# Two hybrid decoder layers on one core: the recurrence begun with its x groups and computed in pairs of tiles, all weight splits on VectorE, P normalised by ScalarE

## The chip, the core and the metric

The kernel runs on one core of a Trainium2 chip. A core has five engines, each with an instruction queue of its own that is worked through in order: TensorE (PE, matmuls; PEld is its weight load), VectorE (DVE), ScalarE (ACT), GpSimd (POOL) and SyncE (SP), which here issues the weight DMAs. They meet through semaphores. The metric is the device time of one execution in microseconds.

## The reference

Two layers of a hybrid decoder run over 264 columns: a prompt of 256 positions and 8 single-step samples. One layer:

```
h = rmsnorm(x);  z = h @ w_in                       # 2048 -> 4096 columns
attn  = sliding-window attention, 16 heads, 4 kv heads, rotary, window 128, a sink per head
lru   = RG-LRU(conv4(x_branch)) * gelu(gate_branch) # 512 wide
sconv = B * conv3(C * h_in)                         # 512 wide
x = x + concat(rmsnorm(attn), rmsnorm(lru), rmsnorm(sconv)) @ w_out
x = x + SwiGLU(rmsnorm(x))                          # 5632 wide
```

The recurrence is `h[t] = a[t]*h[t-1] + sqrt(1-a[t]^2)*i[t]*xc[t]`, with `a` and `i` from sigmoid gates (two small matmuls on the convolved branch `xc`). The attention's probabilities are `p = exp(s - m) / (sum(exp(s - m)) + exp(sink - m))`. Besides the output, the new states of the recurrence, the convolutions and the key and value caches are returned.

## The kernel before

Features lie on partitions in 128-row tiles, the 264 columns in the free dimension. A product with a weight is kept near fp32 by splitting both factors in a high and a low half: three matmuls a tile (`hi*xh`, `hi*xl`, `lo*xh`, lines L152 to L154). Weights stream in as 720 tiles `raw` of 128x1024 (512 KB, five buffers), 360 a layer: 64 for w_in, 32 for w_out, then gate/up and down in three chunks. Each is split: ScalarE casts `hi` (L118), then VectorE subtracts to get `lo` (L122); for 20 of each layer's tiles, every third from 14 to 71, GpSimd does it (L120). Up to four split tiles stand ahead of the product; a split can start when the product has released the buffer four tiles back. One weight tile feeds 24 matmuls, called a block here.

w_in is worked through in 16 groups of four blocks, in the order of `GROUPS` (L41): k, v, the four q heads sets with x and g groups between them, four c groups (the short convolution's C and h), two b groups. A group's result in PSUM is evacuated by VectorE with its RMS scale (`evac`), and starts side work: `attn(i, 0)` and `attn(i, 1)` for each q group (scores L599/L600, maxima L604, Exp L618, P times 1/sum L626, transposes L632, P times V L641/L643), `decode` for the samples, `gelu` and then `lru(c)` for each of the two tiles of a g group, `sconv` for a c group, and `mixnorm` (a norm, then scale and split to the halves `Ba`, `Bl`, `Bs` that w_out reads). Side work is written as generators in queues; after every block `pull` takes one step of each, so `yield n` sets how many blocks later the next step is issued. The four `lru(c)` run one after another, 264 columns at a time, from the x groups' `uxe` and the constants `lsm` (`lru_consts`, a chain of small instructions on four columns). A scheduler then orders each engine's instructions by their dependences and expected times; the rows below show the order that results. w_out (4 groups of 8 blocks) reads `Ba` (attention, k 0 to 7), `Bl` (recurrence, 8 to 11) and `Bs` (short convolution, 12 to 15), in this order. A norm is a sum of squares (`acc`, added up by GpSimd in L186, the short convolution's by VectorE), a product with ones on TensorE (L196), then Ln and Exp on ScalarE and a Newton step on VectorE (L198 to L210).

ScalarE's functions stand in table sets: Ln and Exp of the norm in one, Tanh in another, with a table load (ACT_TABLE_LOAD) where they alternate.

Of the kernel before, what the change touches and what calls it, by code (L numbers as in the profile page):

```python
# [14 lines left out]
P = 128  # L15
# [40 lines left out]
class Kern:  # L56
# [54 lines left out]
    def _split(self):  # L111
# [24 lines left out]
    def linear(self, ngroups, halves, G, xk, evac, alternate=False, before=None):  # L136
        nc = self.nc
        kk = 8 // G
        last = halves * kk - 1
        for g in range(ngroups):  # L140
            ps = [self.MM(alternate and g % 2, j) for j in range(G)]
            for h in range(halves):
# [91 lines left out]
    def run(self):  # L234
# [17 lines left out]
        self.on_pool = {360 * l + j for l in range(DEPTH) for j in range(14, 72, 3)}  # L252
# [14 lines left out]
        self.qp = Queue()  # L267
        self.qbd = self.pers.tile([P, 2, NS, 32], F32, tag="qbd", name="qbd")
# [19 lines left out]
    def prep(self, ks, g, st):  # L288
        """Split x * g for the tiles ks of the next product; their squares go to st."""
# [98 lines left out]
    def mixer(self, l, st, head):  # L388
# [18 lines left out]
        nc.gpsimd.memset(M.che[:, :, 0:2], 0.0)  # L407
# [23 lines left out]
        def setup(ps):  # L431
# [26 lines left out]
            self.lru_consts(l)  # L458
            yield 1
# [13 lines left out]
        def evac(g, ps):  # L473
# [110 lines left out]
    def attn(self, i, p, slot):  # L584
# [119 lines left out]
    def lru_consts(self, l):  # L704
        nc = self.nc
        m = self.lsm
# [19 lines left out]
        self.hba, self.hbi, self.sp2 = hba, hbi, s2  # L726
# [8 lines left out]
    def gelu(self, c, ps):  # L735
# [4 lines left out]
        nc.vector.tensor_tensor(out=t, in0=u, in1=u, op=OP.mult)  # L740
# [259 lines left out]
```

## Time and profile before

| | |
|---|---|
| three runs | 2244.34, 2248.47, 2250.54 us; median 2248.47 |
| profiled execution | span 2247.6 us (the page gives no other time of it) |
| TensorE busy | 2192.0 us (98%) |
| VectorE, ScalarE, GpSimd busy | 1364.4 (61%), 1022.1 (45%), 244.3 us (11%) |
| matmuls, weight loads | 17810 each |
| weight splits | 720 casts on ScalarE; 680 subtractions on VectorE, mean 1235 ns; 40 on GpSimd |
| DMA | 398.33 MB, mean 177 GB/s |

The span runs from the first to the last instruction. A group's row gives the line, the engine, what it writes and reads with the shape, the count, the busy time and the mean of one, and behind the bar the idle time of the engine before it with what ended it. The mixer of layer 0 lies between about 40 and 260 us, that of layer 1 between about 1140 and 1365 us; the rest is w_out and the feed-forward part. The clock column is the clock granted to TensorE, as a share of 2.4 GHz; the lower level is 1.2 GHz.

### The profile page before, as it was taken

What the parts mean: (1) busy time and instruction counts of PE and PEld (TensorE: products, weight loads), DVE (VectorE), ACT (ScalarE), POOL (GpSimd) and SP (SyncE); (2) the same over time, 40 slices, a digit from 0 to 9 for tenths busy, and PEclk for the clock granted to TensorE, in tenths of its full rate; (3) what the DMA queues carried; (4) which work ended last, traced back from release to release, by engine and by line L of the source; (5) the groups of instructions that cost most, each with busy time, mean ns of one, the idle gap of its engine ahead of it and who ended that gap; (6) DMA issues with size and microseconds to landing.
All of it is one profiled execution on the core that took longest, in us unless ns stands there. A gap on an engine that the chain in (4) does not pass through costs nothing.

```text
span 2247.6 us, 42700 instructions
## 1 busy us (share of the span) xinstructions
PE 2192.0 (98%) x17810; PEld 2163.0 (96%) x17810; DVE 1364.4 (61%) x2172; ACT 1022.1 (45%) x1436; POOL 244.3 (11%) x233
## 2 busy tenths in 40 slices
PE   8999899999999999999999899999999999999997
PEld 7989799999999999999999789999999999999997
DVE  7679865555455554555665897565654556545554
ACT  5566554444334443344544665454433444334443
POOL 4324320000000000000123242100000000000002
PEclk9999899999999999999999999999999999999998
DMA  8644555556555555665565345555555555555553
GB/s 294 202 138 128 151 174 186 183 179 180 180 184 179 180 179 184 199 178 180 181 228 170 123 124 170 181 179 184 178 181 182 182 180 179 180 183 181 179 181 102
DMA packets 111617, 398.33 MB, mean 177 GB/s; under 512 B 13312, under 2 KB 15872, under 8 KB 110400
## 3 DMA queue, kind: packets, MB, share of 16 engines
q1 hardware_dynamic: 109840, 389.57, 54.9%
q0 software_dynamic: 864, 4.94, 0.5%
q8 instruction: 139, 2.28, 0.4%
q10 hardware_dynamic: 720, 1.10, 0.1%
q14 instruction: 54, 0.44, 0.1%
HBM read 385.82 MB, written 7.10 MB: 175 GB/s over the span
## 4 chain that ended last, share of the span: by engine, by line
PE 90%; DVE 8%; ACT 1%; DMA 1%; issue 0%; POOL 0%; SPq 0%; DVEq 0%; ACTq 0%
PE mm L152 20%; PE mm L153 20%; PE mm L154 20%; PE pb L154 5%; PE pa L152 5%; PE pa L153 5%; PE pb L152 5%; PE pa L154 4%; PE pb L153 4%; DVE lo L122 1%; DVE Ba L626 1%; DVE Ba L217 1%; DVE lwv L785 0%; DVE la L786 0%; PE pb L632 0%; ACT hi L118 0%
## 5 line engine op out<-in xcount | busy, mean ns | idle before, releaser
L122 DVE TENSOR_TENSOR lo<-raw,hi 128x1024 fp32r<-128x1024 f32 x680 | 838.9, 1235 | 769.4 <-ACT hi L118 769.1
L118 ACT CAST hi<-raw 128x1024 fp32r<-128x1024 f32 x720 | 752.4, 1047 | 991.2 <-PE mm L153 609.1
L152 PE MATMUL mm<-A,hi 128*128 128x264 f32 x2432 | 704.4, 290 | 7.2 <-ACT hi L118 7.2
L154 PE MATMUL mm<-A,lo 128*128 128x264 f32 x2432 | 695.6, 286 | 3.6 <-DVE lo L122 3.6
L153 PE MATMUL mm<-A,hi 128*128 128x264 f32 x2432 | 695.7, 286 | 0.7 <-DVE A L217 0.7
L152 PEld LDWEIGHTS mm<-A,hi 128*128 128x128 f32 x2432 | 462.4, 190 | 15.9 <-issue 8.3
L154 PEld LDWEIGHTS mm<-A,lo 128*128 128x128 f32 x2432 | 461.8, 190 | 6.3 <-DVE lo L122 5.4
L153 PEld LDWEIGHTS mm<-A,hi 128*128 128x128 f32 x2432 | 463.3, 191 | 2.2 <-DVE A L217 1.3
L152 PE MATMUL mm<-Ba,hi 128*128 128x264 f32 x896 | 257.3, 287 | 3.2 <-DVE tab L524 3.2
L154 PE MATMUL mm<-Ba,lo 128*128 128x264 f32 x896 | 257.0, 287 | 3.4 <-DVE lo L122 3.4
L186 POOL TENSOR_TENSOR acc<-acc,t 128x264 f32<-128x264 f32 x79 | 80.3, 1017 | 1651.8 <-ACT t L185 1640.7
L153 PE MATMUL mm<-Ba,hi 128*128 128x264 f32 x896 | 257.2, 287 | 0.0
L152 PE MATMUL pa<-A,hi 128*128 128x264 f32 x704 | 201.4, 286 | 0.0
L154 PE MATMUL pa<-A,lo 128*128 128x264 f32 x704 | 200.5, 285 | 0.0
L154 PE MATMUL pb<-A,lo 128*128 128x264 f32 x704 | 200.4, 285 | 0.0
L153 PE MATMUL pa<-A,hi 128*128 128x264 f32 x704 | 200.2, 284 | 0.0
L152 PE MATMUL pb<-A,hi 128*128 128x264 f32 x704 | 200.1, 284 | 0.0
L153 PE MATMUL pb<-A,hi 128*128 128x264 f32 x704 | 199.9, 284 | 0.0
L154 PEld LDWEIGHTS mm<-Ba,lo 128*128 128x128 f32 x896 | 170.6, 190 | 3.9 <-DVE lo L122 3.8
L152 PEld LDWEIGHTS mm<-Ba,hi 128*128 128x128 f32 x896 | 170.6, 190 | 3.6 <-DVE tab L524 3.6
L153 PEld LDWEIGHTS mm<-Ba,hi 128*128 128x128 f32 x896 | 170.5, 190 | 0.1
L153 PEld LDWEIGHTS pa<-A,hi 128*128 128x128 f32 x704 | 133.8, 190 | 0.0
(263 smaller groups left out, 3324.7 us busy)
## 6 DMA issues: line engine op xcount, KB each, us to landing
raw<-in_wg SPq DMA_DIRECT2D x352, 512.0 KB, 3.6
raw<-in_wd SPq DMA_DIRECT2D x176, 512.0 KB, 3.6
raw<-in_wi SPq DMA_DIRECT2D x128, 512.0 KB, 3.8
raw<-in_wo SPq DMA_DIRECT2D x64, 512.0 KB, 3.8
Bs<-in_kc SPq DMA_DIRECT2D x2, 1024.0 KB, 6.3
out_sk<-Bs POOLq DMA_DIRECT2D x2, 1024.0 KB, 8.4
Bl<-in_vc SPq DMA_DIRECT2D x2, 1024.0 KB, 8.4
q<-t SPq DMA_DIRECT2D x32, 64.0 KB, 2.0
```

The costliest lines, as they stand in the source:

```text
L118: self.nc.scalar.copy(hi, raw)
L122: self.nc.vector.tensor_tensor(out=lo, in0=raw, in1=hi.bitcast(F32), op=OP.subtract)
L152: nc.tensor.matmul(o, hi[:, c:c + P], xh, start=kt == 0, stop=False)
L153: nc.tensor.matmul(o, hi[:, c:c + P], xl, start=False, stop=False)
L154: nc.tensor.matmul(o, lo[:, c:c + P], xh, start=False, stop=kt == last)
L186: (eng or nc.gpsimd).tensor_tensor(out=st["acc"], in0=st["acc"], in1=q, op=OP.add)
L217: self.nc.vector.scalar_tensor_tensor(out=lo, in0=x, scalar=g, in1=hi.bitcast(F32), op0=OP.mult, op1=OP.subtract)
L626: nc.vector.tensor_scalar(pt[g][:, sl], pt[g][:, sl], es[:, c:c + 1], None, OP.mult)
```

## The change

- `GROUPS`: each x group now stands ahead of a q group (k v x q x q g q g q, then c and b), and `lru` starts with the x group, not with the g group behind it.
- `lru(i)` computes two tiles at once: 528 columns an instruction where the form allows it, the two reciprocals and scans apart. It writes `h` to a tile of its own (`lh`); the product with gelu and the square for the norm move to `gelu`'s second half.
- w_out takes its k tiles in another order (`OUT_ORDER`): the recurrence's first, then the attention's, then the short convolution's, and waits only for the two it needs.
- No split on GpSimd: all 720 `lo` on VectorE.
- P is multiplied by 1/sum on ScalarE, and so are gelu's square and the first taps of both convolutions computed there.
- `lru_consts` gets two buffers; layer 1's is issued in the feed-forward part of layer 0, and is free to go anywhere before.

```diff
-GROUPS = [("k", 0), ("v", 0), ("q", 0), ("x", 0), ("q", 1), ("x", 1), ("q", 2), ("g", 0), ("q", 3), ("g", 1),
+GROUPS = [("k", 0), ("v", 0), ("x", 0), ("q", 0), ("x", 1), ("q", 1), ("g", 0), ("q", 2), ("g", 1), ("q", 3),
           ("c", 0), ("c", 1), ("c", 2), ("c", 3), ("b", 0), ("b", 1)]
+OUT_ORDER = (4, 5, 0, 1, 2, 3, 6, 7)
...
-        if j in self.on_pool:
-            self.nc.gpsimd.tensor_tensor(out=lo, in0=raw, in1=hi.bitcast(F32), op=OP.subtract)
-        else:
-            self.nc.vector.tensor_tensor(out=lo, in0=raw, in1=hi.bitcast(F32), op=OP.subtract)
+        self.nc.vector.tensor_tensor(out=lo, in0=raw, in1=hi.bitcast(F32), op=OP.subtract)
...
+        order = order or range(halves)
+        first, last = order[0] * kk, order[-1] * kk + kk - 1
         for g in range(ngroups):
             ps = [self.MM(alternate and g % 2, j) for j in range(G)]
-            for h in range(halves):
+            for h in order:
...
-        self.on_pool = {360 * l + j for l in range(DEPTH) for j in range(14, 72, 3)}
...
-            self.until(lambda: all(k in self.ready for k in range(2 * h + 2)))
+            self.until(lambda: 2 * h in self.ready and 2 * h + 1 in self.ready)
         self.sides.append(self.qp)
-        self.linear(4, 8, 4, self.bh, evac_out, alternate=True, before=before)
+        self.linear(4, 8, 4, self.bh, evac_out, alternate=True, before=before, order=OUT_ORDER)
...
+            if l + 1 < DEPTH:
+                yield 40
+                self.lru_consts(l + 1)
...
+                ql.add(self.lru(i))
             elif kind == "g":
                 for j in range(2):
-                    c = 2 * i + j
-                    self.gelu(c, ps[j])
-                    ql.add(self.lru(c))
+                    self.gelu(2 * i + j, ps[j], ql)
...
-                nc.vector.tensor_scalar(pt[g][:, sl], pt[g][:, sl], es[:, c:c + 1], None, OP.mult)
+                nc.scalar.activation(pt[g][:, sl], pt[g][:, sl], AF.Copy, scale=es[:, c:c + 1])
...
-        m = self.lsm
+        m = self.pers.tile([P, 24], F32, tag="lsm", bufs=2, name=self.nm("lsm"))
...
-    def gelu(self, c, ps):
+    def gelu(self, c, ps, ql):
         nc = self.nc
         u = self.gl[:, c, :]
         nc.vector.tensor_tensor(out=u, in0=ps, in1=self.rs, op=OP.mult)
         t = self.L("lg", 2)
-        nc.vector.tensor_tensor(out=t, in0=u, in1=u, op=OP.mult)
+        nc.scalar.activation(t, u, AF.Square)
         nc.vector.tensor_scalar(t, t, 0.044715, 1.0, OP.mult, OP.add)
         nc.vector.tensor_tensor(out=t, in0=t, in1=u, op=OP.mult)
         nc.scalar.activation(t, t, AF.Tanh, scale=GELU_C)
         def rest():
             nc.vector.scalar_tensor_tensor(out=u, in0=t, scalar=1.0, in1=u, op0=OP.add, op1=OP.mult)
+            nc.vector.scalar_tensor_tensor(out=u, in0=u, scalar=0.5, in1=self.lh[:, c, 0:N], op0=OP.mult, op1=OP.mult)
+            self.norm_add(self.stl, u)
             yield 1
-        self.qp.add(rest())
...
-    def lru(self, c):
+        ql.add(rest())
+    def lru(self, i):
         nc, l = self.nc, self.l
...
+        hba, hbi, sp2 = self.lc[l]
+        cs = (2 * i, 2 * i + 1)
+        col = lambda name, c: self.v(l, name)[:, c:c + 1]
+        pair = lambda tag: self.pers.tile([P, 2, N], F32, tag=tag, name=self.nm(tag))
+        flat = lambda t: t.rearrange("p j n -> p (j n)")
...
+        xc = pair("kab")
+        for j, c in enumerate(cs):
+            ue = self.uxe[:, c, :]
+            nc.scalar.activation(xc[:, j, 0:NP], ue[:, 0:NP], AF.Identity, scale=w[j][:, 0:1], bias=col("lcb", c))
+            for k in range(1, 4):
+                nc.vector.scalar_tensor_tensor(out=xc[:, j, 0:NP], in0=ue[:, k:k + NP], scalar=w[j][:, k:k + 1],
+                                               in1=xc[:, j, 0:NP], op0=OP.mult, op1=OP.add)
...
+        t1, wv = pair("lt1"), pair("lwv")
+        for j, c in enumerate(cs):
+            pr, pi = self.PB()[:, :N], self.PB()[:, :N]
+            nc.tensor.matmul(pr, self.wgate[:, c, :], xc[:, j, :], start=True, stop=True)
+            nc.tensor.matmul(pi, self.wgate[:, 4 + c, :], xc[:, j, :], start=True, stop=True)
+            nc.scalar.activation(t1[:, j, :], pr, AF.Tanh, bias=hba[:, c:c + 1], scale=0.5)
+            nc.scalar.activation(wv[:, j, :], pi, AF.Tanh, bias=hbi[:, c:c + 1], scale=0.5)
+            nc.scalar.activation(t1[:, j, :], t1[:, j, :], AF.Tanh, bias=sp2[:, c:c + 1], scale=sp2[:, c:c + 1])
+            yield 1
+        a, e = xc, pair("vt")
+        nc.vector.scalar_tensor_tensor(out=flat(wv), in0=flat(wv), scalar=1.0, in1=flat(xc), op0=OP.add, op1=OP.mult)
+        nc.vector.tensor_scalar(flat(a), flat(t1), 1.0, None, OP.add)
+        nc.vector.tensor_scalar(flat(t1), flat(t1), 1.0e-30, None, OP.max)
         self.norm_tables()
...
+        nc.scalar.activation(flat(e), flat(t1), AF.Ln)
+        nc.scalar.activation(flat(e), flat(e), AF.Exp, scale=-0.5)
         b0 = self.S()
...
+        nc.vector.reciprocal(a[:, 0, :], a[:, 0, :])
+        yield 1
+        nc.vector.reciprocal(a[:, 1, :], a[:, 1, :])
+        yield 1
...
+        for j, c in enumerate(cs):
+            h = self.lh[:, c, 0:N]
+            nc.vector.tensor_tensor_scan(h[:, 0:NP], a[:, j, 0:NP], wv[:, j, 0:NP], 0.0, OP.mult, OP.add)
...
+        yield 1
...
-        nc.vector.tensor_scalar(y[:, 0:NP], ce[:, 0:NP], w[:, 0:1], None, OP.mult)
+        nc.scalar.activation(y[:, 0:NP], ce[:, 0:NP], AF.Copy, scale=w[:, 0:1])
```

On VectorE, between layer 0's w_in and w_out, the norm of the attention (`nv`) stood in the last tile's recurrence (`lwv`, `lxc`, `la`) and in layer 1's constants (`lsm_12867`):

```order
L712 TENSOR_TENSOR lsm_12867<-lsm_12867,vec 128x4
L795 TENSOR_SCALAR le_2685<-le_2685 128x264
L723 TENSOR_SCALAR lsm_12867<-lsm_12867 128x4
L796 TENSOR_TENSOR lwv_2644<-lwv_2644,le_2685 128x264
L198 TENSOR_SCALAR nv_2775<-pb_2773 128x264
L797 COPY lwv_2644<-s_2691 128x1
L801 TENSOR_TENSOR lxc_2731<-lxc_2731,lwv_2644 128x8
L714 TENSOR_SCALAR lsm_12867<-lsm_12867 128x4
L799 SCALAR_TENSOR_TENSOR lxc_2731<-la_2682,lwv_2644 128x256
L715 RECIPROCAL lsm_12867<-lsm_12867 128x4
L802 SCALAR_TENSOR_TENSOR gl_113<-gl_113,lxc_2731 128x264
L716 TENSOR_TENSOR lsm_12867<-lsm_12867 128x4
```

Now there, with the splits (`lo`) and the sums of squares (`acc`):

```order
L120 TENSOR_TENSOR lo_2824<-raw_2665,hi_2823 128x1024
L120 TENSOR_TENSOR lo_2854<-raw_2701,hi_2853 128x1024
L526 TENSOR_TENSOR tab_2202<-mm_2744,tab_2202 128x264
L526 TENSOR_TENSOR tab_2202<-mm_2745,tab_2202 128x264
L197 TENSOR_SCALAR nv_2892<-pb_2890 128x264
L120 TENSOR_TENSOR lo_2901<-raw_2750,hi_2900 128x1024
L185 TENSOR_TENSOR acc_2884<-acc_2884,t_2887 128x264
L205 TENSOR_TENSOR t_2930<-ne_2894 128x264
L206 TENSOR_TENSOR t_2930<-t_2930,nv_2892 128x264
L207 TENSOR_SCALAR t_2930<-t_2930 128x264
L120 TENSOR_TENSOR lo_2942<-raw_2797,hi_2941 128x1024
L209 TENSOR_TENSOR ra_2934<-ne_2894,t_2930 128x264
```

The recurrence and the constants are gone from it; the norm's four steps (`nv`, `t`, `t`, `ra`) stand between two splits, and then the products `q` with their low halves `Ba`.

On ScalarE, in the third head set of before, P's Exps (`Ba`, `s_1564`) were followed by two casts of splits and by one tile's gates and Ln:

```order
L118 CAST hi_1623<-raw_1453 128x1024
L118 CAST hi_1668<-raw_1489 128x1024
L773 ACTIVATE lt_1663<-pb_1659,lsm_117 128x264
L775 ACTIVATE lwv_1665<-pb_1660,lsm_117 128x264
L776 ACTIVATE lt_1663<-lt_1663,lsm_117 128x264
L783 ACT_TABLE_LOAD
L783 ACTIVATE le_1750<-lt_1663 128x264
L633 COPY Ba_118<-pb_1716 128x384
L633 COPY Ba_118<-pb_1721 128x384
L784 ACT_TABLE_LOAD
L784 ACTIVATE le_1750<-le_1750 128x264
```

In the stretch of the second head set now, behind the same Exps, stand the gates of a tile, a cast, and the multiplications of P among Ln and Exp of the pair (`vt`):

```order
L785 ACTIVATE lt_1343<-pb_1415,lsm_463 128x264
L786 ACTIVATE lwv_1344<-pb_1416,lsm_463 128x264
L787 ACTIVATE lt_1343<-lt_1343,lsm_463 128x264
L119 CAST hi_1464<-raw_1287 128x1024
L628 ACTIVATE Ba_117<-Ba_117,s_1406 128x128
L794 ACT_TABLE_LOAD
L794 ACTIVATE vt_1454<-lt_1343 128x528
L628 ACTIVATE Ba_117<-Ba_117,s_1406 128x256
L795 ACT_TABLE_LOAD
L795 ACTIVATE vt_1454<-vt_1454 128x528
L628 ACTIVATE Ba_117<-Ba_117,s_1406 128x128
L628 ACTIVATE Ba_117<-Ba_117,s_1406 128x256
```

The four multiplications (L628) are new on this engine, and between them lie two table loads.

On VectorE at the kernel's start, layer 0's constants were one chain of `lsm_117`:

```order
L710 TENSOR_SCALAR lsm_117<-vec 128x4
L711 TENSOR_SCALAR lsm_117<-vec 128x4
L712 TENSOR_TENSOR lsm_117<-lsm_117,vec 128x4
L723 TENSOR_SCALAR lsm_117<-lsm_117 128x4
L714 TENSOR_SCALAR lsm_117<-lsm_117 128x4
L715 RECIPROCAL lsm_117<-lsm_117 128x4
```

Now layer 1's (`lsm_5656`) run through them:

```order
L712 TENSOR_SCALAR lsm_463<-vec 128x4
L713 TENSOR_SCALAR lsm_463<-vec 128x4
L711 TENSOR_SCALAR lsm_5656<-vec 128x4
L712 TENSOR_SCALAR lsm_5656<-vec 128x4
L714 TENSOR_TENSOR lsm_463<-lsm_463,vec 128x4
L713 TENSOR_SCALAR lsm_5656<-vec 128x4
L725 TENSOR_SCALAR lsm_463<-lsm_463 128x4
L714 TENSOR_TENSOR lsm_5656<-lsm_5656,vec 128x4
```

Both chains stand before the sixth weight split.

## Rows read from the trace of the kernel before

**Rows 1.** Waits of TensorE, whole run: for whom, us, times, longest

```profile
PE pb L196 <- POOL acc L186: 10.4, 2, 5.3
PE pb L632 <- DVE Ba L626: 8.7, 13, 2.0
...
PE mm L154 <- DVE lo L122: 7.0, 9, 1.7
```

**Rows 2.** Windows by stage: length, busy us by engine (instructions), clock, DMA share

```profile
0.00:40.00 40.00, 29.62 (x206) 27.25 (x207) 33.81 (x66) 27.03 (x49) 20.32 (x26) 1.00 0.78 283
...
130.00:190.00 60.00, 53.98 (x428) 47.71 (x428) 51.92 (x144) 39.12 (x80) 15.91 (x13) 0.94 0.40 125
...
220.00:270.00 50.00, 39.73 (x283) 38.53 (x283) 46.76 (x105) 28.43 (x46) 15.79 (x13) 0.86 0.44 138
...
1240.00:1300.00 60.00, 54.02 (x428) 47.66 (x428) 52.28 (x146) 39.13 (x80) 15.95 (x13) 0.94 0.41 126
...
1330.00:1370.00 40.00, 32.05 (x225) 30.92 (x224) 37.02 (x69) 24.32 (x38) 14.26 (x12) 0.87 0.47 154
1370.00:2228.00 858.00, 858.00 (x7048) 857.93 (x7047) 473.42 (x608) 363.63 (x450) 33.02 (x28) 1.00 0.56 177
2228.00:2247.60 19.60, 5.27 (x34) 4.02 (x33) 9.43 (x18) 2.39 (x6) 4.47 (x5) 0.68 0.29 110
```

**Rows 3.** Timeline of GpSimd, layer 0: start, length, what, idle before

```profile
132.91 2.60 POOL L120 TENSOR_TENSOR lo<-raw,hi 128x1024 fp32r<-128x1024 f32 x1 [8.25 <-ACT hi L118]
...
224.56 2.90 POOL L120 TENSOR_TENSOR lo<-raw,hi 128x1024 fp32r<-128x1024 f32 x1 [6.13 <-ACT hi L118]
```

**Rows 4.** Timeline of VectorE in the same stretches

```profile
133.18 2.48 DVE L626 TENSOR_SCALAR Ba<-Ba,s 128x256 f32<-128x256 f32 x1
135.58 0.42 DVE L785 SCALAR_TENSOR_TENSOR lwv<-lwv,lxc 128x264 f32<-128x264 f32 x1
...
146.86 0.33 DVE L626 TENSOR_SCALAR Ba<-Ba,s 128x256 f32<-128x256 f32 x1
...
225.14 2.34 DVE L712 TENSOR_TENSOR lsm<-lsm,vec 128x4 f32<-128x4 f32 x1
```

**Rows 5.** Groups by form, VectorE, 0 to 380 us: busy, mean ns, idle

```profile
L122 DVE TENSOR_TENSOR lo<-raw,hi 128x1024 fp32r<-128x1024 f32 x88 | 110.7, 1264 | 61.5 <-ACT hi L118 61.4
L626 DVE TENSOR_SCALAR Ba<-Ba,s 128x256 f32<-128x256 f32 x16 | 14.0, 877 | 0.0
...
L785 DVE SCALAR_TENSOR_TENSOR lwv<-lwv,lxc 128x264 f32<-128x264 f32 x4 | 5.8, 1453 | 3.3 <-ACT lwv L775 3.3
L626 DVE TENSOR_SCALAR Ba<-Ba,s 128x128 f32<-128x128 f32 x16 | 4.6, 284 | 0.2
```

**Rows 6.** Chain of waits near 258 us: first and last slow matmul

```profile
257.99 0.22 PE mm L153
...
261.73 0.22 PE mm L152
```

**Rows 7.** Chain of waits: pieces that serve as prices

```profile
8.00 1.73 ACT A L214 x4
...
27.46 1.24 DVE lo L122
...
124.16 0.43 PE pa L599 x4
...
131.06 0.46 PE pb L770 x2
...
1238.97 1.38 ACT Ba L618 x6
```

**Rows 8.** Timeline of ScalarE around a table load

```profile
210.54 1.04 ACT L118 CAST hi<-raw 128x1024 fp32r<-128x1024 f32 x1
211.59 1.28 ACT L773 ACT_TABLE_LOAD   x1
212.89 0.48 ACT L773 ACTIVATE lt<-pb,lsm 128x264 f32<-128x264 f32 x1
```

More of the change, by code (lines that the diff above doesn't have):

```diff
@@ L134, in _next, with linear @@
         return r
-    def linear(self, ngroups, halves, G, xk, evac, alternate=False, before=None):
+    def linear(self, ngroups, halves, G, xk, evac, alternate=False, before=None, order=None):
         nc = self.nc
         kk = 8 // G
-        last = halves * kk - 1
+        order = order or range(halves)
+        first, last = order[0] * kk, order[-1] * kk + kk - 1
         for g in range(ngroups):
             ps = [self.MM(alternate and g % 2, j) for j in range(G)]
-            for h in range(halves):
+            for h in order:
                 if before:
@@ L151, in linear @@
                         o = ps[m][:, :N]
-                        nc.tensor.matmul(o, hi[:, c:c + P], xh, start=kt == 0, stop=False)
+                        nc.tensor.matmul(o, hi[:, c:c + P], xh, start=kt == first, stop=False)
                         nc.tensor.matmul(o, hi[:, c:c + P], xl, start=False, stop=False)
                         nc.tensor.matmul(o, lo[:, c:c + P], xh, start=False, stop=kt == last)
-                if h == halves - 1:
+                if h == order[-1]:
                     evac(g, [p[:, :N] for p in ps])
@@ L241, in run @@
             srcs += [I["wi"][l, j] for j in range(64)]
-            srcs += [I["wo"][l, j] for j in range(32)]
+            srcs += [I["wo"][l, 8 * g + h] for g in range(4) for h in OUT_ORDER]
             go = do = 0
@@ L399, in mixer @@
         M.gl = pt([P, 4, N], "gl")
-        M.che = pt([P, 4, 268], "che")
+        M.lh = pt([P, 4, 268], "che")
         M.tab = pt([P, 4, N], "tab")
         M.stage = pt([P, 216], "stage")
-        M.lsm = pt([P, 24], "lsm")
         M.scr = pt([P, 4224], "Ba")
@@ L516, in evac @@
                     M.yc = pt([P, 4, N], "tab")
+                    M.che = pt([P, 4, 268], "che")
+                    nc.gpsimd.memset(M.che[:, :, 0:2], 0.0)
                 t = self.T()
@@ new lines, in lru @@
+        yield 1
+        xc = pair("kab")
[5 more added lines that the diff above has]
+                                               in1=xc[:, j, 0:NP], op0=OP.mult, op1=OP.add)
+            s = self.S()
+            nc.vector.tensor_reduce(out=s, in_=prs[j], axis=AX.X, op=OP.add)
+            nc.vector.tensor_scalar(xc[:, j, NP:N], s, col("lcb", c), None, OP.add)
+            yield 1
@@ L782, in lru @@
+        a, e = xc, pair("vt")
+        nc.vector.scalar_tensor_tensor(out=flat(wv), in0=flat(wv), scalar=1.0, in1=flat(xc), op0=OP.add, op1=OP.mult)
+        nc.vector.tensor_scalar(flat(a), flat(t1), 1.0, None, OP.add)
+        nc.vector.tensor_scalar(flat(t1), flat(t1), 1.0e-30, None, OP.max)
         self.norm_tables()
-        nc.scalar.activation(e, t1, AF.Ln)
-        nc.scalar.activation(e, e, AF.Exp, scale=-0.5)
-        nc.vector.scalar_tensor_tensor(out=wv, in0=wv, scalar=1.0, in1=xc, op0=OP.add, op1=OP.mult)
@@ new lines, in lru @@
+        yield 1
+        nc.vector.tensor_tensor(out=flat(wv), in0=flat(wv), in1=flat(a), op=OP.mult)
+        nc.vector.tensor_scalar(flat(a), flat(a), 2.0, -1.0, OP.mult, OP.add)
+        nc.vector.tensor_tensor(out=flat(t1), in0=flat(t1), in1=flat(e), op=OP.mult)
+        nc.vector.tensor_tensor(out=flat(wv), in0=flat(wv), in1=flat(t1), op=OP.mult)
+        yield 1
+        nc.vector.tensor_tensor(out=flat(e), in0=flat(e), in1=flat(t1), op=OP.mult)
+        nc.vector.tensor_scalar(flat(e), flat(e), -0.5, 1.5, OP.mult, OP.add)
@@ new lines, in lru @@
+        nc.vector.tensor_tensor(out=flat(wv), in0=flat(wv), in1=flat(e), op=OP.mult)
+        nc.vector.tensor_copy(wv[:, :, 0], b0[:, 0:2])
+        yield 1
+        for j, c in enumerate(cs):
+            h = self.lh[:, c, 0:N]
+            nc.vector.tensor_tensor_scan(h[:, 0:NP], a[:, j, 0:NP], wv[:, j, 0:NP], 0.0, OP.mult, OP.add)
+            nc.vector.tensor_tensor(out=h[:, NP:N], in0=a[:, j, NP:N], in1=self.v(l, "h0")[:, 8 * c:8 * c + 8],
+                                    op=OP.mult)
+            nc.vector.tensor_tensor(out=h[:, NP:N], in0=h[:, NP:N], in1=wv[:, j, NP:N], op=OP.add)
+            nc.gpsimd.tensor_copy(self.stage[:, 9 * c:9 * c + 9], h[:, NP - 1:N])
```

56 lines of the change are left out of this document (8 added, 48 removed).

## The prediction

> **What bounds the kernel now.** I read the waits of TensorE first. Three carry most of the time it loses: the ones-product of a norm (`pb` L196) waits for GpSimd's sum of squares, the transposes of the attention's P (L632) wait for VectorE's multiplication of P (L626), and matmuls wait for the low half of a weight split (`lo`) [rows 1]. All three stand in the mixers. The windows by stage show it: TensorE idles 40.00 - 29.62 = 10.4 us at the start and 14.3 us at the tail, which the change hardly touches; between 1370 and 2228 us it never idles, and 858.00 us / 7048 gives 0.122 us a matmul, so 2.92 us for a block of 24. In the mixers it idles 6.0 us (130:190), 10.3 (220:270), 6.0 (1240:1300) and 8.0 (1330:1370), 30.2 us in sum, and there VectorE is busy 52 of 60 and 47 of 50 us [rows 2]. So TensorE is the bound over the whole run, and VectorE, in order, is what it waits for in these four stretches.
>
> Why VectorE is late shows when its timeline is laid beside GpSimd's. GpSimd's weight split runs 132.91 to 135.51 and 224.56 to 227.46 us [rows 3]. VectorE's multiplication of P, 0.33 us at 146.86, takes 2.48 us when it meets the first of them, and an operation on four elements a lane takes 2.34 us under the second [rows 4]. A split on GpSimd holds up certain VectorE instructions until it is over. In the groups by form the wide L626 has a mean of 877 ns and L785 one of 1453 ns [rows 5], against 0.33 and 0.42 undisturbed [rows 4].
>
> The clock adds to it. After such an idle stretch the chain shows matmuls 0.22 us apart, from 257.99 to 261.95 us [rows 6], where 0.122 is usual: the lower of the two levels. Those 4.0 us hold 1.8 us of loss. Clock times busy gives at most 0.06 x 54.0 + 0.14 x 39.7 + 0.06 x 54.0 + 0.13 x 32.1 = 16 us in the four stretches [rows 2]; part of the low clock falls into idle time, so I take 12. **What a perfect mixer could give back is 30.2 + 12 = 42 us.**
>
> **The change part by part.**
>
> *Splits back on VectorE, P on ScalarE.* A layer puts 20 splits of 1.24 us [rows 7] on VectorE, 24.8 us. It takes off P's multiplications, 14.0 + 4.6 = 18.6 us, and the holds that L785 shows, 4 x (1.45 - 0.42) = 4.1 us [rows 4, 5]. Three kinds of one-input pass (gelu's square, the first taps of both convolutions), 12 instructions of about 0.33, are another 4 us. Pairing halves the number of the recurrence's instructions and doubles their length; I count it as nothing. That is -2 us net; other forms under GpSimd's splits are held too and would make it more. So VectorE's total hardly falls. What counts is where its work stands.
>
> *The recurrence earlier.* Before, the last tile's recurrence runs at 216 to 229 us, with layer 1's constants (`lsm`) among it, and the norm after it is the wait of 5.3 us in each layer [rows 1]. Behind it on VectorE queue the attention's norm, eight products and their low halves, the evacuation of the last w_in group and the splits: hence the rest of the 10.3 us. In the new order the recurrence's norm product stands after block 39 instead of 57, and the constants of both layers run at the start. The attention's norm product stands after block 59, five blocks (14.6 us) behind the last P times V. Between lie one copy and seven squares on ScalarE (8 x 0.43 = 3.4 us, priced by the four passes in 1.73 us [rows 7]) and seven additions, which the five blocks cover even at 1.5 us each: no wait. w_out now begins with the recurrence's two blocks and needs the attention only at block 66, 20 us after the product, against some 12 us of work (eight casts at 0.43, sixteen VectorE passes at about 0.42, the norm). I cost the transition at nothing; this cover is the weight matmuls, and if it is gone the 5.3 us come back.
>
> The evacuations, GpSimd's small convolution copies and SP's four q transfers change places by one group of four blocks, 11.7 us. SP's q transfers of a head come behind one more weight load each; the first scores move from block 14 to block 18 with them, so nobody waits longer. Layer 1's constants before the sixth split: 13 more instructions in a chain that ended with a `lo` on the critical chain at 27.46 us [rows 7]. The two chains interleave, each in the other's latency: 0.5 us, between 0 and 13 of the shortest form shown, 13 x 0.28 = 3.6 [rows 5].
>
> *What stays late.* (a) Blocks 19 to 22: both P of the first head pair pass ScalarE behind the split of block 23. Cast 1.0, eight Exps at 0.46 (six pieces, three Exps with their reads, 1.38 us [rows 7]), cast 1.0, two multiplications 0.7, so 6.4 us, against scores 0.86 and two blocks 5.84 on TensorE, 6.7: a wait of 1 us, 0 to 3 if VectorE is behind with the maxima. (b) Blocks 27 to 30 are the worst. ScalarE from the end of block 27: cast 1.0, two squares 0.9, two table loads 2.6 [rows 8], two Tanh 0.9, Exps 1.9, three gate passes 1.3, cast 1.0, multiplication 0.3, load 1.3, Ln over 528 0.7, multiplication 0.4: 12.2 us to the first pair of P; then load, Exp, two multiplications, 2.7 us more, to 14.9. TensorE meanwhile has two sets of scores (0.43 for one half, as much for the other), gates 2 x 0.46 [rows 7] and three blocks, 11.4 us. So it waits 0.8 us, transposes 0.3, and waits 2.4 again: 3 us. Bounds 0 (passes overlap, none of the VectorE operands late) and 6 (ScalarE waits once for VectorE's sums or maxima, as P's Exps do today). The multiplication on ScalarE is priced by a pass with a per-lane scale, 0.43; the trace shows none on P.
>
> The Trainium skill (ScalarE: Activation LUTs, "What ACT_TABLE_LOAD costs") counts a drain of about 1.38 us on top of the 1.28 us load at each switch of table sets. The trace disagrees: the load at 211.59 begins 0.01 us after the cast ends and the next pass 0.02 us after the load [rows 8]. By the page, the four loads of (b) would add 5.5 us a layer and the time would be 2232.
>
> *Sum.* Left over per layer: (a) 1, (b) 3, small waits for P's halves elsewhere 1, one stretch at the lower clock 2: 7 us, 14 in both. Start 0.5. The gain is 42 - 14 - 0.5 = 27.5 us. The profiled execution spans 2247.6 us, the page gives no other time of it, and the median of the runs, 2248.5, lies 0.9 above: 2220.1 + 0.9 = **2221 us**.
>
> **Rivals.** *Nothing is left late*: (a) and (b) vanish since ScalarE's passes overlap and the order leaves slack. For it: ScalarE is busy only 39 of 60 us at 130:190 [rows 2]; against it: the sum in (b). 2248.5 - 41.5 = 2207.
>
> *ScalarE takes VectorE's place.* It gets 16 wide and 16 narrow multiplications, squares and taps, about 15 us a layer, less three table loads. Each cast of a split waits behind them. If (a), (b) and the second head's transposes near block 42 cost 3, 6 and 3 us a layer with the lower clock after each (1.8), 2 x (12 + 5.4) = 35 of the 42 us stay: 2241. For it: 47 us of ScalarE work between blocks 20 and 36 in my tally, against 16 blocks, 47 us, and the attention's own products on TensorE; against it: those products, and three blocks of split buffered ahead.
>
> *Slower: the holds are not GpSimd's.* Then the long instructions stay and VectorE gets 24.8 us of splits against 16 x (0.33 + 0.28) + 4 = 14 us taken off: 11 us more a layer, decisive once a stretch holds more VectorE work than time, as at 220:270 with 46.8 of 50 us. Half of it on the path gives 2248.5 + 11 = 2259. Against it: two coincidences as clean as those of rows 3 and 4. By the Trainium skill (SBUF — State Buffer, "Who interferes with whom") VectorE and GpSimd take a shared port pair as an exclusive lock for a whole instruction; that is what these rows show, and it halves this rival's chance.
>
> **How the numbers follow.** Forecast 0.56, nothing late 0.20, ScalarE bound 0.18, holds not GpSimd's 0.06. About 0.3%, 6.7 us, is what a measurement of this kernel can tell from no change. The first two are faster; the third lies at that edge (2241.7), half faster, half the same; the fourth is slower but for one part in six. So faster 0.85, same 0.10, slower 0.05. The range begins below the second case, by the 16 us bound of the clock: 2248.5 - 46 = 2202, and ends at the third, 2241: what lies beyond is the fourth and half of the third.
>
> **What would show it.** TensorE's wait for GpSimd's `acc` in the mixer gone; the wide DVE forms back at 0.3 to 0.5 us, with no VectorE instruction of 2.4 us; VectorE below 47 of 50 us at 220:270; TensorE's largest mixer wait then that of the P transposes for ScalarE, largest at the second head's first pair; clock 1.00 around 230 to 262 us. The forecast is wrong if `hi` casts come late for the matmuls, if the first 40 us lose over 2 us, or if the idle time of the mixers stays above 25 us.

## The result, and the profile after

The changed kernel takes 2210.35 us, median of four runs (2209.31 to 2212.66), against 2247.35 us (2244.34 to 2250.54) on the same chip: a ratio of 0.9833, 95% interval 0.9821 to 0.9844. The prediction said 2221 us, 2202 to 2241, and faster. The profiled execution took 2212.66 us, the slowest of the four, and spans 2210.9 us, 36.7 us less than before.

TensorE's largest waits in the kernel after, whole run (for whom, us in total, times, longest):

```profile
PE mm L151 <- ACT hi L119: 6.4, 1, 6.4
PE pb L634 <- ACT Ba L628: 3.6, 2, 1.8
PE mm L151 <- DVE t L465: 1.8, 1, 1.8
PE pa L601 <- DMA q<-t: 1.8, 1, 1.8
PE mm L153 <- DVE lo L120: 1.1, 1, 1.1
```

The wait for `acc` of [rows 1] is gone, and so is that of the transposes for VectorE; in its place stands one wait for ScalarE's P per layer, 1.8 us. The 6.4 us are the start, which was there before (6.3). The windows that answer to [rows 2]; layer 1 now runs 18 us earlier (length, busy us by engine with instructions, clock, DMA share, GB/s):

```profile
0.00:40.00 40.00, 30.28 (x198) 28.35 (x199) 34.53 (x88) 27.20 (x50) 19.56 (x24) 0.96 0.76 280
70.00:80.00 10.00, 8.20 (x57) 7.49 (x56) 8.87 (x18) 4.28 (x5) 0.00 (x0) 0.84 0.93 346
120.00:130.00 10.00, 8.19 (x54) 7.59 (x53) 9.59 (x20) 8.18 (x13) 0.00 (x0) 0.83 0.34 107
130.00:190.00 60.00, 59.53 (x517) 54.95 (x516) 45.66 (x123) 42.31 (x101) 9.43 (x15) 1.00 0.50 150
...
220.00:270.00 50.00, 49.90 (x406) 49.55 (x405) 39.68 (x70) 31.11 (x47) 6.14 (x7) 1.00 0.56 171
1206.00:1262.00 56.00, 54.02 (x449) 50.17 (x448) 45.38 (x110) 42.68 (x93) 8.35 (x12) 0.97 0.49 143
```

At 130:190 and 220:270, where TensorE idled 6.0 and 10.3 us, it now idles 0.5 and 0.1 us, at full clock. VectorE is busy 39.7 of 50 us in the latter instead of 46.8. The order of the groups has changed, so a window no longer holds the same work. Over the whole mixer of layer 0 TensorE idled 17.0 us and now idles 4.2, of which 3.6 stand at 70:80 and 120:130 (before, then after):

```profile
40.00:270.00 230.00, 213.00 (x1679) 200.37 (x1679) 179.66 (x441) 128.83 (x240) 76.78 (x74) 0.96 0.50 165
40.00:270.00 230.00, 225.81 (x1832) 215.16 (x1832) 172.87 (x386) 149.16 (x290) 33.62 (x60) 0.99 0.56 179
```

Line 1 of the page for the kernel after (busy us, share of the span, instructions):

```profile
PE 2180.1 (99%) x17810; PEld 2155.4 (97%) x17810; DVE 1334.2 (60%) x2076; ACT 1043.5 (47%) x1510; POOL 144.6 (7%) x193
```

TensorE runs the same 17810 matmuls in 11.9 us less (2192.0 - 2180.1), which I put down to the clock (0.86 to 0.94 in the four mixer windows of [rows 2], 0.97 to 1.00 in the windows that answer to them), and idles 30.8 us of its span instead of 55.6: 24.8 us. Together that is the 36.7 us. VectorE did 40 more splits and yet is busy 30.2 us less (1364.4 - 1334.2).

### The profile page after: what moved, and what is told of

It reads as the page before. It is cut to its first block, busy times and chain, and to the rows that moved or that the text cites. A ratio compares the mean times of both kernels' runs of the same rounds, so it can differ in the third digit from the quotient of the medians.

```text
span 2210.9 us, 42662 instructions
## 1 busy us (share of the span) xinstructions
PE 2180.1 (99%) x17810; PEld 2155.4 (97%) x17810; DVE 1334.2 (60%) x2076; ACT 1043.5 (47%) x1510; POOL 144.6 (7%) x193
## 4 chain that ended last, share of the span: by engine, by line
PE 93%; DVE 2%; DMA 2%; ACT 2%; issue 0%; SPq 0%; POOL 0%; DVEq 0%; POOLq 0%; ACTq 0%
PE mm L151 21%; PE mm L152 21%; PE mm L153 21%; PE pb L153 5%; PE pa L151 5%; PE pa L153 5%; PE pa L152 5%; PE pb L151 5%; PE pb L152 5%; DMA raw<-in_wi 1%; DVE lo L120 1%; PE pb L634 1%; PE pa L643 0%; DMA q<-t 0%; DVE A L216 0%
## 5 line engine op out<-in xcount | busy, mean ns | idle before, releaser
L120 DVE TENSOR_TENSOR lo<-raw,hi 128x1024 fp32r<-128x1024 f32 x720 | 889.7, 1238 | 778.2 <-ACT hi L119 777.2
L152 PE MATMUL mm<-Ba,hi 128*128 128x264 f32 x896 | 254.8, 284 | 0.0
L151 PE MATMUL mm<-Ba,hi 128*128 128x264 f32 x896 | 254.6, 284 | 0.0
```

Of the source, the lines that this page charges most:

```text
L151: nc.tensor.matmul(o, hi[:, c:c + P], xh, start=kt == first, stop=False)
```

## The experiments

The change has three parts: the splits taken off GpSimd (S), the recurrence with its orders (R), and P with a few passes on ScalarE (P). I took them apart first. The first four versions below ran on one chip with each other, and so did each later set.

**One part undone, one part alone.** `e1_gpsimd_splits_back` (R and P):

```diff
-        self.nc.vector.tensor_tensor(out=lo, ...)
+        if j in self.on_pool: self.nc.gpsimd.tensor_tensor(out=lo, ...)   # 20 of a layer's 360
+        else: self.nc.vector.tensor_tensor(out=lo, ...)
```

> The changed kernel with the 40 weight splits (20 a layer) put back on GpSimd, nothing else. Theory (a GpSimd split holds VectorE; the gain is the end of the holds plus the earlier recurrence): VectorE loses 2 x 24.8 us of splits but its wide passes in the mixer show 2.3 to 2.5 us again when they meet a split, and TensorE's idle time in the two mixers rises from about 6 us to 10 to 18; time 2210 + 8 = 2218 (2213 to 2225). Rival 1 (only the order of the recurrence and of w_out counts): 2210 within 2. Rival 2 (VectorE's total work is what counts): 25 us less a layer on VectorE, so faster than 2210.

`e2_splits_alone` (S): the reverse of that edit, in the kernel before.

> The kernel before with all 720 splits on VectorE, nothing else. Theory: no VectorE pass of 2.3 us or more is left, the wide multiplication of P falls from a mean of 877 ns to about 330, TensorE's wait of the transposes for it from 21.7 us to about 8, the wait for acc (10.4 us) stays in part; 2247 - 12 = 2235 (2229 to 2242). Rival 1 (order alone): 2247 within 3, the wait for acc as before. Rival 2 (the holds are not GpSimd's): long passes stay and VectorE has 24.8 us more a layer: 2259.

`e3_p_on_vectore` (S and R; gelu's square and the taps stay on ScalarE):

```diff
-                nc.scalar.activation(pt[g][:, sl], pt[g][:, sl], AF.Copy, scale=es[:, c:c + 1])
+                nc.vector.tensor_scalar(pt[g][:, sl], pt[g][:, sl], es[:, c:c + 1], None, OP.mult)
```

> The changed kernel with P multiplied by VectorE again (64 passes), nothing else. Theory: without holds these passes cost 0.33 and 0.28 us, 10 us a layer spread over 190 us in which VectorE is under 80% busy, and ScalarE's late pair (the 3.6 us wait of the transposes for P) goes or becomes a wait for VectorE of the same size: 2210 + 2 (2207 to 2215). Rival 3 (P on ScalarE is the main gain): 2225 or more, with transposes waiting 10 us or more for VectorE.

`e4_old_recurrence` (S and P): the kernel before with those two parts' lines of the diff.

> The kernel before with all splits on VectorE and with P, gelu's square and the convolutions' first taps on ScalarE, but with the old order of groups, the old recurrence tile by tile and the old order of w_out: the change without its recurrence part. Theory: the stall at the passage to w_out stays for the most part (wait for acc about 8 of 10.4 us, plus the stretch at the low clock behind it): 2210 + 14 = 2224 (2218 to 2231). Rival 1 (order alone is the gain): 2240 or more. Rival 3 (P and splits are all of it): 2210 within 3.

Then the two parts that were still missing alone, `e7_recurrence_alone` (R) and `e8_scalare_alone` (P):

> The recurrence part of the change alone (order of groups, pairs, order of w_out, constants with two buffers): 40 splits stay on GpSimd, and P, gelu's square and the first taps on VectorE. Theory: the parts work on one cost, VectorE's lateness under the holds, so their gains don't add; the recurrence leaves the holds on P: 2248 - 16 = 2232 (2226 to 2240), with transposes waiting 8 us or more for P on VectorE. Rival 4 (the parts add: the recurrence is worth the 6 us by which it beat the splits alone): 2242 (2239 to 2245).

> The ScalarE part alone: the kernel before with P, gelu's square and the first taps on ScalarE, splits on GpSimd, old recurrence and orders. Theory: P no longer meets the holds, so the 8.7 us of TensorE's wait for it mostly go, the stall at the passage to w_out stays: 2248 - 9 = 2239 (2232 to 2245). Rival 4 (the parts add: without holds, P on ScalarE was worth -1 to +4 us): 2247 to 2252.

| parts | us, median (runs) | ratio to before (95%) | TensorE idle | VectorE busy |
|---|---|---|---|---|
| none | 2248.62 (2242.72 to 2250.02) | | 55.6 | 1364.4 |
| P | 2244.59 (2242.11 to 2246.07) | 0.9986 (0.9977 to 0.9996) | 51.9 | 1334.8 |
| R | 2223.53 (2223.02 to 2224.22) | 0.9900 (0.9884 to 0.9915) | 40.7 | 1352.5 |
| R, P | 2224.83 (2222.37 to 2227.01) | 0.9900 (0.9885 to 0.9915) | 39.0 | 1320.4 |
| S | 2212.12 (2212.06 to 2215.67) | 0.9849 (0.9831 to 0.9867) | 33.0 | 1360.1 |
| S, P | 2211.05 (2209.96 to 2211.28) | 0.9838 (0.9823 to 0.9853) | 32.5 | 1339.3 |
| S, R | 2205.98 (2205.37 to 2207.47) | 0.9817 (0.9803 to 0.9832) | 28.8 | 1346.1 |
| S, R, P | 2210.35 (2209.31 to 2212.66) | 0.9833 (0.9821 to 0.9844) | 30.8 | 1334.2 |

Each ratio is to the kernel before in the same set of runs; the first row has its runs in the set of `e5` to `e8` (the median in that of `e1` to `e4` is 2248.40). That kernel's runs spread over 6 to 8 us in every set, those of the others over 1 to 5, so I compare versions of one set by their own medians, and a comparison between sets is less sure. The last row is the changed kernel's first runs, the row above the last differs from it by 64 passes on P alone. The splits alone bring 36 us, within the intervals as much as the whole change. The recurrence brings 25 us while GpSimd still splits, and 6 us once it does not: both work on VectorE's lateness, and it can be taken away only once. P on ScalarE brings 4 us in the kernel before (the interval of its ratio ends at 0.9996), about 1 us beside S, and by the medians of two sets it costs 4.4 us beside S and R, where I had expected it to bring 2. So my theory of `e2` and `e4`, that the stall at the passage to w_out belongs to the old recurrence, fell: `e2` takes 2212, not 2235, and `e4`, which keeps that recurrence, takes 2211, not 2224. `e1`, at 2225, lies at the upper end of its range. TensorE's waits in `e2_splits_alone`:

```profile
PE mm L149 <- ACT hi L118: 7.0, 2, 6.1
PE pb L193 <- POOL acc L183: 5.0, 2, 2.5
PE mm L151 <- DVE lo L119: 4.1, 6, 1.1
...
PE pb L628 <- DVE Ba L622: 0.4, 2, 0.2
```

The wait for `acc` halves (10.4 to 5.0) with nothing done to the recurrence, and that for P goes from 8.7 to 0.4 us with P still on VectorE (the 21.7 us that the expectation gives for it stand in no list). P's two forms there, whole run (busy us, mean ns, idle before them):

```profile
L622 DVE TENSOR_SCALAR Ba<-Ba,s 128x256 f32<-128x256 f32 x32 | 11.0, 345 | 0.0
L622 DVE TENSOR_SCALAR Ba<-Ba,s 128x128 f32<-128x128 f32 x32 | 10.0, 313 | 0.4
```

877 ns [rows 5] became 345. The sum over all forms is the number to keep: `e2` has 40 splits of 1.24 us more on VectorE, 49.6 us, and VectorE is busy 4.3 us *less* (1364.4 - 1360.1). By this difference GpSimd's 40 splits had held it for some 54 us (49.6 + 4.3), to save it 49.6.

`e7` took 2224 where I had expected 2232 and the other theory 2242. The wait for `acc` is gone there, but the transposes still wait for P on VectorE, 7.3 us instead of 8.7:

```profile
PE pb L638 <- DVE Ba L632: 7.3, 4, 2.7
```

In the new order P's wide passes seldom meet a split (a mean of 343 ns), but others do: L836, 128x256, has a mean of 1157 ns, against 479 in `e3`. Without holds VectorE would be busy about 1304 us in `e7`, an estimate from `e3` (1346.1, less 49.6 for 40 splits, and 8 for the 24 passes that `e3` has on ScalarE); it is busy 1352.5. So the recurrence does not remove the holds, some 48 us are left; TensorE waits less for the passes that they now fall on.

`e8` was nearer 2245 than 2239. Its P waits fell from 8.7 to 2.1 us (last line), but the gates' products now wait for ScalarE and VectorE (second and third lines; the first is what stays at the passage):

```profile
PE pb L196 <- POOL acc L186: 9.7, 2, 4.9
...
PE pb L771 <- ACT Ba L680: 4.9, 2, 2.5
...
PE pb L770 <- DVE lxc L762: 2.3, 2, 1.2
PE pb L632 <- ACT Ba L626: 2.1, 6, 0.4
```

**Is it really a hold?** In `e1` the low halves themselves come from GpSimd, 2.5 us each on average instead of 1.24, so lateness of `lo` could be the cause. The trace of the kernel before speaks against it: TensorE never waits for a `lo` of GpSimd there (L120), and although ScalarE's casts wait 9.9 us for such halves, TensorE waits only 0.9 us for `hi` outside the start. Two versions leave every `lo` on VectorE and give GpSimd useless work at the same 40 places.

```diff
+        if j in self.on_pool:   # e5_gpsimd_reads
+            self.nc.gpsimd.tensor_tensor(out=self.junk, in0=raw[:, 0:704], in1=hi.bitcast(F32)[:, 0:704],
+                                         op=OP.subtract)
...
+        if j in self.on_pool:   # e6_gpsimd_writes
+            self.nc.gpsimd.tensor_copy(self.junk[:, 0:1], hi.bitcast(F32)[:, 0:1])
+            for n in (704, 704, 352):
+                self.nc.gpsimd.memset(self.junk[:, 0:n], 0.0)
```

> The changed kernel with all 720 low halves on VectorE as they are, and beside them, for the 40 weight tiles that GpSimd split before, a useless subtraction on GpSimd that reads 704 of the tile's 1024 columns from raw and hi (about 1.65 us each, 2.4 x 704/1024) and writes a spare tile. Nothing that TensorE reads is computed later. Theory (a GpSimd instruction that reads SBUF holds VectorE): VectorE passes of 1 us or more appear again where 0.3 to 0.5 stood, and the time is 2210 + 10 (2216 to 2228). Rival L (in the kernel before, the low halves themselves came late from GpSimd): 2210 within 2. Rival Q (GpSimd's own sums come late behind the extra work): 2215 to 2222, no longer VectorE passes, and the same in the run whose extra work only writes.

> The changed kernel with the same 40 places filled by GpSimd work that reads one column of hi and then only writes: three memsets of 704, 704 and 352 columns, about 1.7 us in sum. Theory: work that only writes holds no VectorE pass, the passes keep 0.3 to 0.5 us; what is left is the delay of GpSimd's own sums: 2210 + 2 (2209 to 2215). Rival Q: the same as the run whose extra work reads. Rival L: 2210 within 2.

`e5` takes 2226.97 us (ratio 0.9915, 0.9899 to 0.9931), `e6` 2211.63 (0.9847, 0.9832 to 0.9863). GpSimd is busy as long in the one as in the other, 246.5 and 248.5 us; but the one that reads takes 15.3 us more in the same set (16.6 and 1.3 us above the changed kernel's first runs). VectorE's forms in `e5`, 0 to 380 us:

```profile
L610 DVE CUSTOM_DVE_ANT_0 Ba<-pa,con 128x256 f32<-128x256 f32 x16 | 6.7, 417 | 0.0
L560 DVE TENSOR_TENSOR q<-q,ra 128x264 f32<-128x264 f32 x8 | 4.4, 594 | 0.0
...
L794 DVE SCALAR_TENSOR_TENSOR lwv<-lwv,kab 128x528 f32<-128x528 f32 x2 | 3.1, 1550 | 0.4 <-ACT lwv L790 0.4
L209 DVE TENSOR_SCALAR t<-t 128x264 f32<-128x264 f32 x5 | 3.0, 607 | 0.1
```

and the same forms in `e6`:

```profile
L612 DVE CUSTOM_DVE_ANT_0 Ba<-pa,con 128x256 f32<-128x256 f32 x16 | 6.7, 418 | 0.0
...
L562 DVE TENSOR_TENSOR q<-q,ra 128x264 f32<-128x264 f32 x8 | 3.0, 426 | 0.0
...
L211 DVE TENSOR_SCALAR t<-t 128x264 f32<-128x264 f32 x5 | 1.5, 301 | 0.1
L796 DVE SCALAR_TENSOR_TENSOR lwv<-lwv,kab 128x528 f32<-128x528 f32 x2 | 1.4, 724 | 0.4 <-ACT lwv L792 0.4
```

Forms with SBUF operands alone are held (594 against 426 ns, 1550 against 724, 607 against 301); the maxima, which read scores from PSUM and only the mask from SBUF, take 417 and 418, and one that runs wholly inside a GpSimd read (from 83.04 us in `e5`, inside the first read shown below) takes 0.42. The Trainium skill (SBUF — State Buffer, "Who interferes with whom") says so of the first two forms: two SBUF inputs on VectorE contend with a GpSimd instruction that reads SBUF, not with one that only writes. The trace agrees, with 594 and 1550 ns where GpSimd reads and 426 and 724 where it almost only writes. The third form, L209, has one SBUF input, so that sentence does not cover it.

The hold goes both ways. GpSimd in `e5`, and one column of 128 rows read by GpSimd in `e6`:

```profile
83.03 1.71 POOL L122 TENSOR_TENSOR junk<-raw,hi 128x704 bf16<-128x704 f32 x1
...
107.17 2.73 POOL L122 TENSOR_TENSOR junk<-raw,hi 128x704 bf16<-128x704 f32 x1 [2.65 <-ACT hi L119]
```

```profile
103.21 1.24 POOL L122 CAST junk<-hi 128x1 bf16<-128x1 f32 x1 [3.86 <-ACT hi L119]
```

VectorE's split of the same tile, in `e5` and in `e6`:

```profile
107.12 1.22 DVE L120 TENSOR_TENSOR lo<-raw,hi 128x1024 fp32r<-128x1024 f32 x1 [1.70 <-ACT hi L119]
```

```profile
103.17 1.23 DVE L120 TENSOR_TENSOR lo<-raw,hi 128x1024 fp32r<-128x1024 f32 x1 [2.62 <-ACT hi L119]
```

Where VectorE began 0.05 us earlier, GpSimd's 1.71 us became 2.73, and one column took 1.24 us, until VectorE's 1.23 us were over. One thing the pair does not separate: the three memsets let GpSimd's own sums pass between them, the one long subtraction does not, so some of the 16.6 us is GpSimd's queue (VectorE waited 2.31 us for `acc` near 223 us in `e5`, 1.54 near 219 in `e6`). That the reads keep the split's buffers longer is not what costs: TensorE waits 6.2 us for `hi` in both and 2.4 and 2.1 us for `lo`; what grows from `e6` to `e5` is its wait for VectorE's evacuation `tab` (0.2 to 5.7 us) and for P (4.2 to 7.2). The pair was run in the changed kernel, where the splits on GpSimd cost 14.5 us (`e1`). That the same hold makes up the 36 us in the kernel before rests on its forms and busy times, not on such a pair.

**What is left.** Three versions of `e3`, and the changed kernel with `e9`'s edit:

```diff
-        m = self.pers.tile([P, 24], F32, tag="lsm", bufs=2, ...)   # e9, e10, e12
+        m = self.pers.tile([P, 24], F32, tag="lsm", bufs=1, ...)
-        yield 3 + slot                                             # e10
+        yield 3 + slot + (i == 0)
-OUT_ORDER = (4, 5, 0, 1, 2, 3, 6, 7)                               # e11
+OUT_ORDER = tuple(range(8))
```

> The changed kernel with P on VectorE (the version that gave 2206) and with one buffer for the recurrence's constants instead of two, so that layer 1's cannot be computed at the kernel's start. Theory: TensorE's wait of 1.8 us for a rotated k half behind the two chains of constants goes (VectorE was busy 10.0 of 10 us at 30 to 40), nothing is late elsewhere since VectorE has 10 us free in the 50 us where the constants stood before: 2206 - 2 = 2204 (2202 to 2206). Rival (the two chains hide in each other's latency; the wait is the rotation's own): 2206 within 1, the wait stays.

> The version with one buffer of constants, and besides the first head set's scores one block (2.9 us) later. Theory: TensorE's wait of 1.9 us for the DMA of q in layer 0, and part of the stretch at a clock of 0.84 behind it, go; the attention ends one block later, which the blocks before w_out's attention part cover: 2 us less than the version before it (2200 to 2204). Rival (the first head set is on a chain that ends in w_out): no faster, with a new wait of w_out's matmuls for Ba or of the norm.

> The changed kernel with P on VectorE, and w_out's k tiles in their old order: attention first, then the recurrence, then the short convolution. Theory (the new order is what gives the attention's norm its time): the attention's last product ends about 12 us after its norm product behind block 59, while its first halves are wanted at block 64, 14.6 us after: a wait of 0 to 3 us a layer, and a stretch at the low clock with it: 2206 + 4 (2206 to 2213). Rival (with the holds gone the order does not matter): 2206 within 1.5.

> The changed kernel as it is (P on ScalarE) with one buffer for the recurrence's constants: against the version with P on VectorE and one buffer (2203.67 us) it differs in P alone. Theory (P on ScalarE costs what its late pair makes TensorE wait, 1.8 us a layer, and the stretch at the lower clock behind it): 2203.7 + 4 = 2208 (2206 to 2210), with the wait of the transposes for ScalarE as before, 1.8 us a layer. Rival (the 4.4 us between the two P versions came from the start, where the layer's constants stand): 2204 within 1.

`e9` is the fastest: 2203.67 us (2203.59 to 2204.24), 0.9807 (0.979 to 0.9825). The largest of TensorE's waits in it, without the start's:

```profile
PE mm L153 <- DVE lo L120: 2.6, 5, 1.1
PE pb L634 <- DVE Ba L628: 1.9, 4, 0.7
PE mm L151 <- DVE t L465: 0.9, 1, 0.9
```

The wait for the rotated k half is halved, and the one for q's DMA is gone with it, so the premise of `e10` was gone too. `e10` takes 2208.46 (2206.33 to 2209.21), 4.8 us more: no faster, as its rival said, but by a wait that neither had named, of the transposes for P of a head set, 2.0 us a layer:

```profile
PE pb L634 <- DVE Ba L628: 4.0, 2, 2.0
```

`e11` takes 2205.97 (2205.55 to 2206.80) against 2205.98 of `e3` in another set: w_out's order is worth nothing here, with the holds gone. `e12` takes 2208.21 (2207.74 to 2209.49), as expected, with this wait:

```profile
PE pb L634 <- ACT Ba L628: 3.6, 2, 1.8
```

So by the medians P on ScalarE costs 4.4 and 4.5 us, whether the constants stand at the start or not. Both comparisons are between two sets, and the intervals of the ratios overlap; the runs themselves do not, and between the traces of `e9` and `e12` TensorE idles 2.2 us more (29.7 against 27.5) and is busy 1.5 us longer (2176.4 against 2174.9).

## Why the prediction was right, and where it was wrong

The time came out inside the range, and the holds are the cause that the prediction named. Which edit brings the gain it did not see: it put the splits back "-2 us net" and gave the passage to the recurrence, while the splits alone bring 36 of the 37 us. That the sum came near in spite of this is partly luck: either edit alone takes away most of the idle time at the passage.

*What bounds the kernel.* Right: VectorE's lateness in the mixers under GpSimd's splits. Its ceiling for a perfect mixer, 42 us, was a little low: `e9` spans 2202.4 us, 45.2 less than before, of which 28.1 are idle time (55.6 - 27.5) and 17.1 clock. The term of 30.2 us was not reached, that of 12 was too small.

*The holds.* The mechanism was right, and the rival that the holds are not GpSimd's is excluded by `e2`, which should then have been slower than before, and by `e5` and `e6`. The size was wrong. The step counted the holds of P and of L785 and came to "-2 us net" a layer for VectorE; it fell by 15 us a layer (30.2 / 2). The holds are 27 us a layer (53.9 / 2, from `e2`): many forms with SBUF operands meet a split, and the step priced two; "other forms under GpSimd's splits are held too" stood there without a number. With 27 in it the step's own sum comes near: 24.8 of splits - 27 of holds - 10.5 for P without holds (21.0 / 2, from `e2`) - 4 for the other passes = -17.

*The recurrence earlier.* The forecast that the passage to w_out costs nothing came true (0.1 us of idle at 220:270), and clock 1.00 with it. Its reason was only half of it: the prediction gave the whole 10.3 us to the place of the recurrence and to w_out beginning with it. With the old recurrence and the old orders `e2` waits 2.5 us a layer for `acc`, and between 190 and 270 us it idles 3.5 us (30.00 - 27.49 and 50.00 - 49.05) where the kernel before idled 10.3:

```profile
190.00:220.00 30.00, 27.49 (x216) 26.52 (x215) 28.28 (x69) 19.35 (x30) 12.21 (x12) 0.98 0.56 176
220.00:270.00 50.00, 49.05 (x389) 48.61 (x389) 44.93 (x97) 30.77 (x50) 7.50 (x10) 0.98 0.52 161
```

The recurrence alone (`e7`), with the holds still there, leaves 2.4 us:

```profile
220.00:270.00 50.00, 47.59 (x385) 47.06 (x384) 38.71 (x63) 28.20 (x43) 17.60 (x14) 1.00 0.53 163
```

Either edit alone takes away two thirds of that idle time or more, so it cannot be shared out between them; by `e11` w_out's order is worth nothing once the holds are gone.

*(a) and (b).* (a) was 0 instead of 1 us. (b) was 1.8 instead of 3 us a layer, at the place named. ScalarE after, layer 0 (start, length, what):

```profile
112.05 1.28 ACT L188 ACT_TABLE_LOAD   x1
113.34 1.28 ACT L745 ACT_TABLE_LOAD   x1
114.64 0.74 ACT L745 ACTIVATE lg<-lg 128x264 f32<-128x264 f32 x2
...
119.82 1.28 ACT L794 ACT_TABLE_LOAD   x1
121.11 0.65 ACT L794 ACTIVATE vt<-lt 128x528 f32<-128x528 f32 x1
121.66 0.50 ACT L628 ACTIVATE Ba<-Ba,s 128x256 f32<-128x256 f32 x1
122.18 1.28 ACT L795 ACT_TABLE_LOAD   x1
123.47 0.64 ACT L795 ACTIVATE vt<-vt 128x528 f32<-128x528 f32 x1
124.02 0.79 ACT L628 ACTIVATE Ba<-Ba,s 128x128 f32<-128x128 f32 x2
```

From the cast at 110.35 the first pair of P is through after 11.8 us (12.2 predicted) and the second after 14.5 (14.9). TensorE's own work there, from 110.37 to the first transposes at 122.08, took 11.7 us (11.4 predicted), so the first wait, 0.8 us, did not come, and the second was 1.8 instead of 2.4. TensorE's transposes of the second pair:

```profile
124.46 1.09 PE L634 MATMUL pb<-con,Ba 128*128 128x128 f32 x3 [1.81 <-ACT Ba L628]
```

They start at 124.46, 1.81 us late. Each load is followed by its pass within 0.02 us, and the one at 122.18 begins 0.02 us after the pass before it: the drain that the Trainium skill (ScalarE: Activation LUTs, "What ACT_TABLE_LOAD costs") adds is again not in the trace. That P on ScalarE is a loss on the whole, 4.4 us, might have been seen from this sum: it was put among the costs of the change and never held against P's 10.5 us a layer on a VectorE no longer late.

*The start.* "0.5 us" was somewhat too small. The two chains of constants fill VectorE at 30 to 40 us and the rotated k half comes 1.8 us late. VectorE was nearly as full there before, and TensorE idled too (before, then after):

```profile
30.00:40.00 10.00, 9.03 (x74) 8.84 (x74) 9.85 (x25) 6.59 (x7) 4.08 (x4) 1.00 0.85 296
30.00:40.00 10.00, 8.16 (x68) 7.98 (x67) 10.00 (x32) 6.72 (x8) 3.14 (x3) 1.00 0.83 281
```

So the chains cost 0.9 us of idle time more (1.84 - 0.97). The lower clock of the first 40 us (0.96) does not follow from them: `e1` and `e6` have both chains at the start and 1.00. `e9`, which takes one chain away, is 2.3 us below `e3` (two sets), with half of this wait and the whole of the next gone.

*"The first scores move with them, so nobody waits longer."* Wrong by 1.1 us: the wait for q's DMA went from 0.7 to 1.8 us, with a clock of 0.84 in that stretch (70:80).

*The clock.* Taken as 12 us before, with 16 as the bound; between before and `e9` the same matmuls differ by 17.1 us (2192.0 - 2174.9), so the bound was the better value. Part of the 17.1 is the kernel before's own spread: its runs in the set of `e5` to `e8` go from 2242.72 us at a mean clock of 0.994 to 2250.02 at 0.990. The prediction's own sum was 19.7 us of idle (30.2 - 10 - 0.5) and 8 of clock (12 - 4); measured were 24.8 and 11.9. The error of 9 us between the spans lies half in waits that did not come and half in the clock. The step from the span to the time, 0.9 us in the sum, is 1.8 for the changed kernel (2212.66 - 2210.9).

*The rivals.* The result, 2210, lies between the forecast and "nothing is left late" (2207), nearer to the latter, though (b), which should then have vanished, is there with 1.8 us a layer. "ScalarE takes VectorE's place" is right in sign for P alone, by a tenth of the 42 us.

## What to carry to other kernels

Work given to GpSimd that reads SBUF is not free for VectorE even when GpSimd is mostly idle (11% busy here): compare VectorE's forms, instruction by instruction, with and without the offload, and count what all of them are held for, not the two longest groups. Where several edits attack one lateness, their gains don't add; run each alone, since the one that does all of it may be the simplest line. Before a stage is moved to another engine to relieve the first, ask whether the first is still late after the other edits.

## What the runs showed of the hardware that was not expected

- 40 subtractions of 128x1024 on GpSimd held VectorE for some 54 us in sum (by the difference of its busy times in `e2`), more than the 49.6 us they take on VectorE.
- GpSimd is held by VectorE in the same way: a read of one column took 1.24 us beside a VectorE subtraction of 1.23 us, and 0.19 us at its shortest (81.24 us, `e6`).
- A pass with a single SBUF input and an immediate (L209, 128x264) is held too, 607 against 301 ns; one with its wide input in PSUM is not, 417 against 418 ns.
